# An RWKV and attention hybrid layer on one core: the triangular inverse before the power, the output pool in another place, attention's units in another order

## The chip, the core and the metric

The kernel runs on one core of a Trainium2 chip. TensorE (PE; its weight loads are PEld) multiplies, VectorE (DVE), ScalarE (ACT) and GpSimd (POOL) do the rest, SyncE (SP) issues most of the DMAs. Each engine takes its own instructions in the order that was fixed when the program was built. The metric is the device time of one execution in microseconds; the median of three runs before the change is 2141.12 us (2139.89 to 2146.02).

## The reference

One layer on x of 2048 tokens by 1024, in f32, and a last norm:

```
xn = rmsnorm(x);  p = xn @ w_in                  # 1024 -> 3076 columns
# RWKV-7, 8 heads of 64: one state S (64x64) per head, token after token
S = S*w_t + (S @ -kk_t) (kk_t*a_t)^T + v_t k_t^T;   y_t = S r_t
y_rwkv = (groupnorm(y) + (r.k.r_k) v) * silu(gate)
# sparse attention, 8 heads: an indexer scores all earlier keys,
# the best 256 of each query are kept, softmax over these
score = sum_h w_h relu(qi_h . ki);  idx = top_k(score, 256)
y_attn = softmax(q . c[idx]) @ c[idx], through w_uk, w_uv, * silu(gate)
out = rmsnorm(x + concat(y_rwkv, y_attn) @ w_out)
```

## The kernel before

Four stages, each a Python function; the program is unrolled.

`phase_as` does the projections (three f32r products for each f32 one) and the picker, which writes one mask per query block to DRAM. It is not touched.

`phase_r` does the RWKV heads. Tokens are taken in 16 batches of 128, each of two chunks of 64 (`o` = 0, 1); the heads stand side by side. A batch n goes through
- `prep` (twice, for two halves of the heads): loads, decays on VectorE, the products `E` of the chunk with itself, masked by VectorE (L978); at its end GpSimd scales `BK` (L988), queued behind the last operation of an inverse (`scaled_after`);
- `systems`: the triangular systems in `E` go through DRAM (`du`, L1016) into `A` (L1018), which has one buffer;
- `inverse`: GpSimd inverts them in 31 steps of two operations on `Xr` and `Xtmp` (L1032, L1034); `Xr` goes through DRAM (`dx`, L1035) into `TT` (L1039);
- `chain`, for each `o`: TensorE reads the state, ScalarE copies, TensorE solves with `TT` (L1069) in two steps, and VectorE writes the next state `S` (L1097); `y` is copied (L1098);
- `tail_norm`: the group norm of y on VectorE and ScalarE, with a power on GpSimd (`gst`, L1113) and a last multiply on VectorE (L1114); `tail_out`: transposes, `yo` on ScalarE and GpSimd (L1127 to L1130), a store to `d_y`.

In the loop over n the order of the source is: `tail_norm` of batch n-1, `inverse` of n+1 (queued on GpSimd behind that power), the first `prep` of n+2, `chain(n, 0)`, `tail_out` of n-1, second `prep` of n+2 and its `systems`, `chain(n, 1)`.

`phase_t` does the attention: for each of 4 pairs of heads p, 16 query blocks b, one unit each. `scores` makes the scores of a unit in chunks of 512 keys (L1262, L1263; VectorE adds the mask and takes the maximum, L1264; ScalarE exponentials, L1271), and beside it `attend` does the unit before: transposes (L1295), copies (L1297), products with the values (L1304), times the gate (L1317), then a store. A unit b has b+1 key tiles of 128; a head pair has 136, all four 544. Units run b = 0 to 15. A chunk of keys is loaded when the first unit needs it (`b % 4 == 0`), queries for two blocks at a time.

`phase_w` does the output: weights split into `wh` and `wl`, then 16 blocks of 128 tokens: load `yl`, copy to `yh`, difference, 48 products of 512 columns (L1377 to L1380), the sum with x, the norm, the store.

A planner sets the order on each engine at build time: an instruction goes in when its operands are ready by the planner's own estimate, the lowest priority number first. `with later(n)` adds to that number: the chain comes first, the rest of `phase_r` next, attention behind that with `later(2)`, the output with `later(3)`. `with tc.issue_after(x)` queues what it holds behind `x` on `x`'s engine. Tiles lie in pools, left and right; a pool that takes the place of another waits for its tiles. Before the change attention (pool `pT`) takes the left place when the picker's pool is closed, and the output (`pW`) takes `pT`'s place:

```
        with ExitStack() as sl:
            env["pa"], env["ps"] = pools(sl, "pT", "left")
            with later(2):
                phase_t(env)
        env["pa"], env["ps"] = pools(left, "pW", "left")
```

Of the kernel before, what the change touches and what calls it, by code (L numbers as in the profile page):

```python
# [20 lines left out]
NB = 16  # L21
# [3 lines left out]
NP = 4  # L25
# [11 lines left out]
def kernel(ctx: ExitStack, tc: tile.TileContext, x, norm_g, w_in, mu_shift, w0, w_up, a0, a_up,  # L37
# [109 lines left out]
    with ExitStack() as left, ExitStack() as right:  # L147
        env = dict(locals())
        with ExitStack() as sl:
            env["ps_"], env["pss"] = pools(sl, "pS", "left")  # L150
            with ExitStack() as sr:
                env["pa"], env["ps"] = pools(sr, "pX", "right")
                phase_as(env)
            sr = right.enter_context(ExitStack())
            if "R" in stages:
                env["pr"], env["psr"] = pools(sr, "pR", "right")
                phase_r(env)
        with ExitStack() as sl:
            env["pa"], env["ps"] = pools(sl, "pT", "left")
            with later(2):  # L160
                phase_t(env)
        env["pa"], env["ps"] = pools(left, "pW", "left")
        V.tensor_reduce(any_bad, bad, axis=AX.X, op=OP.max)
        rows = env["ps"].tile([128, 512], F32, name="rows", tag="po", bufs=3)
        PE.matmul(rows[0:1, 0:1], any_bad, ones1, start=True, stop=True)
        V.tensor_scalar(flag, rows[0:1, 0:1], 0.5, None, op0=OP.is_gt)
        with later(3):
            phase_w(env)
    redo = nc.values_load(flag, min_val=0, max_val=1)
    with tc.If(redo > 0):  # L170
        again(env)
# [716 lines left out]
def phase_r(env):  # L888
# [43 lines left out]
    def prep(tq, i, eC, scaled_after):  # L932

        sl = slice(tq * W, tq * W + W)
        u = NS(dict(ps=(i, 2 + i), sl=sl, i=i))
        ld = tl([128, 5, NC, C], F32, "ld", 2)
        u.vt = tl([128, 2, C + W], F32, "vt", 4)
        dma(ld.rearrange("p q (g o) c -> p q g (o c)", g=2),
            e.d_rw.rearrange("p q (g i) t -> p q g i t", i=2)[:, :, :, i, sl])
        v = e.d_v4.rearrange("p (g i) t -> p g i t", i=2)[:, :, i]  # L940
        if tq:
            dma(u.vt, v[:, :, tq * W - C:tq * W + W])
        else:
# [24 lines left out]
        V.tensor_tensor(u.X[:, :, 1], r, eL[:, :, 1:], op=OP.mult)  # L968
        u.E = tl([128, 2, NC, 2 * C], F32, "E", 6)
        mk = mask[:, i].rearrange("p a b -> p (a b)")[:, None, :].to_broadcast([128, NC, 2 * C])  # L970

        pe = [pst([128, NC, 2 * C], "rp", 2) for h in range(2)]
        for c in range(NC):
            for h in range(2):
                PE.matmul(pe[h][:, c], u.BK[HALF[h], c].rearrange("p a b -> p (a b)"),  # L975
                          u.X[HALF[h], c].rearrange("p a b -> p (a b)"), start=True, stop=True)
        for h in range(2):
            V.tensor_tensor(u.E[:, h], pe[h], mk, op=OP.mult)  # L978
        for p, hf in zip(u.ps, half):
            V.scalar_tensor_tensor(r[:, hf], r[:, hf], e.rkc[:, p:p + 1], k[:, hf], op0=OP.mult, op1=OP.mult)  # L980

        pb = pst([128, 2, W], "rp", 2)
        PE.matmul(fl(pb), fl(hsum), fl(u.r), start=True, stop=True)
        u.bv = tl([128, 2, W], F32, "bv", 6)
        V.tensor_tensor(u.bv, pb, u.vt[:, :, C:], op=OP.mult)
        bk = u.BK.rearrange("p c a b -> p c (a b)")
        with tc.issue_after(scaled_after):
            G.tensor_tensor(bk, bk, u.eC[:, :, None].to_broadcast([128, NC, 2 * C]), op=OP.mult)  # L988
        return u
# [127 lines left out]
    def tail_out(us, y):  # L1117
# [2 lines left out]
        for c in range(NC):  # L1120
            PE.transpose(pt[:, c].rearrange("p a b -> p (a b)"), y[:, c], ident)
        for i, u in enumerate(us):
            yo = tl([128, 2, W], F32, "yo", 3)
            gr = tl([128, 2, W], F32, "gr", 2)
            dma(gr, e.d_gr4.rearrange("p (g i) t -> p g i t", i=2)[:, :, u.i, u.sl])
            for g, p in enumerate(u.ps):
                S.activation(yo[:, g].rearrange("p (a b) -> p a b", a=2), pt[:, 2 * g:2 * g + 2, i], AF.Identity,  # L1127
                             scale=e.gng[:, p:p + 1], bias=e.gnb[:, p:p + 1])
            G.tensor_tensor(yo, yo, u.bv, op=OP.add)
            G.tensor_tensor(yo, yo, gr, op=OP.mult)  # L1130
            dma(e.d_y.rearrange("p (g i) t -> p g i t", i=2)[:, 0:2, u.i, u.sl], yo)
# [28 lines left out]
    for n in range(N):  # L1160
        b = batch.pop(n)
        new = batch[n + 2] = begin(n + 2) if n + 2 < N else None
        nx = batch.get(n + 1)
        norm = None
        with e.later():
            if b0:
                norm = tail_norm(y0)
            if nx:
                with behind(norm):
                    nx.TT, first = inverse(nx.A)  # L1170
            if new:
                with behind(state):
                    new.us.append(prep(n + 2, 0, new.eC, first))
        y = tl([128, NC, 128], F32, "y", 2)
        state = chain(b.us, b.TT, b.eC, y, n, 0)
        with e.later():
            if b0:
                tail_out(b0.us, y0)
            if nx:
                for u in nx.us:  # L1180
                    prep2(u)
            if new:
                with behind(state):
                    new.us.append(prep(n + 2, 1, new.eC, first))
                new.A = systems(new.us)
        state = chain(b.us, b.TT, b.eC, y, n, 1)
        y0, b0 = y, b
    with e.later():
        tail_norm(y0)
# [3 lines left out]
def phase_t(env):  # L1193
# [23 lines left out]
    def chunk_in(p, c):  # L1217
# [6 lines left out]
        dma(v, e.d_vt[:, 4 * c:4 * c + 4, p])  # L1224
        KT[p, c], VT[p, c] = k, v

    def queries_in(p, c):

        Q[p, c] = []
        for i in range(2):  # L1230
            q = tl([128, 2, 256], F32R, f"q{i}", 2)
            for s in range(2):
                dma(f32(q)[HALF[s]], e.d_q[i][:, p, c * 256:c * 256 + 256].rearrange("(h d) t -> d h t", h=2))
            Q[p, c].append(q)

    def load(p, b):

        if b % 4 == 0:
            chunk_in(p, b // 4)
        if b % 2 == 0:  # L1240
            queries_in(p, b // 2)
        mk = MK[p, b] = tl([128, T], BF16, "mk", 3)
        dma(mk[:, :(b + 1) * 128], e.d_mask[b])
        ga = GA[p, b] = tl([128, 128], F32, "ga", 5)
        return dma(ga, e.d_ga[p][:, b * 128:b * 128 + 128]).ins

    def scores(p, b, out):

        n = (b + 1) * 128
        mk = MK.pop((p, b))  # L1250
        qs = slice(b % 2 * 128, b % 2 * 128 + 128)
        qh, ql = Q[p, b // 2]
        rows = [tl([128, T], F32, "sc", 4) for h in range(2)]
        mx = tl([128, 2, 8], F32, "mx", 3)
        sums = tl([128, 2], F32, "sums", 3)
        for nt, c0 in enumerate(range(0, n, C)):
            w = min(C, n - c0)
            wp = max(w, 256)
            k = KT[p, nt]
            for h in range(2):  # L1260
                pS = pst([128, C], "s", 2)
                PE.matmul(pS[:, :wp], qh[:, h, qs], k[:, h, :wp], start=True, stop=False)  # L1262
                PE.matmul(pS[:, :wp], ql[:, h, qs], k[:, h, :wp], start=False, stop=True)  # L1263
# [4 lines left out]
        nt = (n + C - 1) // C  # L1268
        for h in range(2):
            V.tensor_reduce(mx[:, h, 4:5], mx[:, h, :nt], axis=AX.X, op=OP.max, negate=True)  # L1270
            S.activation(rows[h][:, :n], rows[h][:, :n], AF.Exp, bias=mx[:, h, 4:5], accum_out=sums[:, h:h + 1])  # L1271
        out.extend((rows, sums))

    def attend(p, b, rows, sums):
# [42 lines left out]
        V.tensor_tensor(ga, ga, po, op=OP.mult)  # L1317
        stores.append((e.d_y[:, 4 + p, ts], ga))

    units = [(p, b) for p in range(NP) for b in range(NB)]  # L1320
    last, stores = None, []
    load(*units[0])
    for i, u in enumerate(units + [None]):
        out = []
# [14 lines left out]
    for x in stores:  # L1339
        dma(*x)  # L1340


def phase_w(env):
# [18 lines left out]
    for tb in range(NB):  # L1362
# [2 lines left out]
        yr = tl([128, 8, 128], F32, "yl", 2)  # L1365
        yl = yr.bitcast(F32R)
        dma(yr, e.d_y[:, :, ts])
        S.activation(yh, yr, AF.Copy)  # L1368
        V.tensor_tensor(yl, yr, f32(yh), op=OP.subtract)
        xr = tl([128, D], F32, "xr", 2)  # L1370
        dma(xr, e.x[0, ts, :])
# [44 lines left out]
```

## Time and profile before

| | |
|---|---|
| median of three runs | 2141.12 us |
| the profiled execution | 2145.71 us, span 2144.0 us |
| busy: PE, PEld, DVE, ACT, POOL | 1818.9, 1435.7, 1313.2, 1022.5, 800.7 us |
| mean granted TensorE clock | 0.901 |
| up to about 975 us | projections and picker |
| 975 to 1843 us | RWKV heads, attention between them |
| 1843 to 1938 us | the rest of attention |
| 1957 to 2144 us | output |

Times are microseconds from the start of the span. L1069 is line 1069 of the kernel. Busy times of TensorE contain modelled ends, so packed products overlap in them. In the chain of waits each row is what the work stood on at that time; "issue" is time for which the profile shows no cause.

### The profile page before, as it was taken

Reading aid. Unit: us, or ns where it says so; the run is one execution under the profiler, and the core shown is the slowest. Engines: PE = TensorE matmul, PEld = TensorE weight load, DVE = VectorE, ACT = ScalarE, POOL = GpSimd, SP = SyncE. Lnnn points to the kernel's source line nnn. Section 1 sums busy time; section 2 is a strip of 40 time slices with the busy share of each in tenths; the row PEclk is TensorE's granted clock in tenths of the full one; section 3 lists DMA queues with packets and bytes.
Section 4 is the critical chain, followed back from the end, with each engine's and each line's share of the span. In section 5 each row is a group of like instructions: output and inputs, shape, how many; then the busy total and the mean of one; then the engine's idle time right before and its main releaser. Section 6 shows DMA issues by size and latency. Waiting matters only on the chain.

```text
span 2144.0 us, 36181 instructions
## 1 busy us (share of the span) xinstructions
PE 1818.9 (85%) x12906; PEld 1435.7 (67%) x12906; DVE 1313.2 (61%) x3050; ACT 1022.5 (48%) x1966; POOL 800.7 (37%) x1925
## 2 busy tenths in 40 slices
PE   5798998789797988895797977898787888996998
PEld 4676776568575766774576755677566666775886
DVE  5533539879697988985475665665466563543332
ACT  5323593444535654332364653556445555663221
POOL 1100233452545355541555554544455454100000
PEclk9788999989898999997898997999688897998999
DMA  7536243233352433227643553335433433214443
GB/s 252 187 135 200 66 136 126 81 110 95 112 181 78 138 125 118 90 83 182 169 113 97 129 147 92 106 98 145 115 105 95 108 93 101 85 39 162 145 148 110
DMA packets 309038, 262.50 MB, mean 122 GB/s; under 512 B 82544, under 2 KB 258288, under 8 KB 307696
## 3 DMA queue, kind: packets, MB, share of 16 engines
q1 hardware_dynamic: 304464, 248.03, 39.6%
q0 software_dynamic: 4384, 12.06, 1.7%
q8 instruction: 104, 1.70, 0.3%
q14 instruction: 86, 0.70, 0.1%
HBM read 166.37 MB, written 97.85 MB: 123 GB/s over the span
## 4 chain that ended last, share of the span: by engine, by line
PE 26%; DMA 11%; POOL 9%; issue 7%; DVE 4%; ACT 2%; SPq 1%; POOLq 0%; DVEq 0%; ACTq 0%
DMA dx<-Xr 5%; PE tr L1295 4%; PE om L1304 3%; POOL Xr L1034 3%; POOL Xtmp L1032 3%; PE po L1377 3%; PE po L1378 3%; PE po L1380 3%; PE s L1262 2%; PE s L1263 2%; DMA TT<-dx 2%; PE ch L1069 1%; DMA q<-d_q 1%; PE rp L975 1%; DMA d_y<-ga 1%
## 5 line engine op out<-in xcount | busy, mean ns | idle before, releaser
L578 PE MATMUL pm<-xh,wh 128*128 128x512 f32 x800 | 327.8, 410 | 19.8 <-DVE t L589 10.5
L579 PE MATMUL pm<-xl,wh 128*128 128x512 f32 x800 | 324.6, 406 | 0.0
L580 PE MATMUL pm<-xh,wl 128*128 128x512 f32 x800 | 324.1, 405 | 0.0
L1264 DVE CUSTOM_DVE_ANT_0 sc<-s,mk 128x512 f32<-128x512 f32 (+3 forms) x320 | 188.7, 607 | 161.2 <-PE s L1263 127.6
L1297 ACT ACTIVATE pt<-tr 128x512 f32<-128x512 f32 (+1 forms) x288 | 158.4, 570 | 142.2 <-PE tr L1295 81.6
L578 PEld LDWEIGHTS pm<-xh,wh 128*128 128x128 f32 x800 | 156.6, 196 | 60.7 <-DVE t L589 12.7
L1295 PE MATMUL tr<-ident,sc 128*128 128x128 f32 x1088 | 182.4, 295 | 8.5 <-ACT pt L1297 7.5
L579 PEld LDWEIGHTS pm<-xl,wh 128*128 128x128 f32 x800 | 156.5, 196 | 35.1
L580 PEld LDWEIGHTS pm<-xh,wl 128*128 128x128 f32 x800 | 155.9, 195 | 35.7
L1304 PE MATMUL om<-pt,vt 128*64 128x128 f32 x2176 | 172.8, 296 | 7.4 <-DVE ga L1287 7.3
L1271 ACT ACTIVATE sc<-sc,mx 128x128 f32<-128x128 f32 (+15 forms) x128 | 153.0, 1197 | 36.5 <-DVE mx L1270 35.9
L1032 POOL TENSOR_TENSOR Xtmp<-Xr,A 128x60 f32<-128x60 f32 (+24 forms) x496 | 148.6, 300 | 55.3 <-DMA A<-du 18.1
L1262 PE MATMUL s<-kt,q 128*128 128x512 f32 (+2 forms) x320 | 152.2, 477 | 17.4 <-DVE mx L1264 13.2
L1034 POOL TENSOR_TENSOR Xr<-Xr,Xtmp 128x60 f32<-128x60 f32 (+24 forms) x496 | 149.0, 300 | 37.1
L1295 PEld LDWEIGHTS tr<-ident,sc 128*128 128x128 f32 x1088 | 134.2, 150 | 40.1 <-issue 12.8
L1304 PEld LDWEIGHTS om<-pt,vt 128*64 128x64 f32 x2176 | 134.8, 147 | 35.2 <-issue 17.0
L318 ACT ACTIVATE mk<-x,st 128x1920 bf16<-128x1920 f16 (+5 forms) x72 | 98.0, 1361 | 105.1 <-POOL st L315 105.0
L250 ACT ACTIVATE rl<-lg,wi 128x512 f32<-128x512 f32 (+3 forms) x152 | 94.1, 631 | 100.3 <-PE lg L248 51.7
L1263 PE MATMUL s<-kt,q 128*128 128x512 f32 (+2 forms) x320 | 126.8, 398 | 7.8 <-DMA q<-d_q 7.7
L1069 PE MATMUL ch<-R,TT 32*32 32x64 f32 x1024 | 53.3, 242 | 92.0 <-DMA TT<-dx 91.6
L321 DVE TENSOR_SCALAR_CACHE_REDUCE mk<-x,st 128x2048 bf16<-128x2048 f16 (+5 forms) x72 | 120.6, 1676 | 1.4
L1377 PE MATMUL po<-wh,yh 128*128 128x512 f32 x256 | 100.9, 394 | 19.4 <-ACT yh L1368 19.4
(329 smaller groups left out, 3899.5 us busy)
## 6 DMA issues: line engine op xcount, KB each, us to landing
wraw<-in_w_in_dram SPq DMA_DIRECT2D x42, 512.0 KB
d_rw<-t SPq DMA_DIRECT2D x80, 256.0 KB
ld<-d_rw SPq DMA_DIRECT2D x32, 640.0 KB
q<-d_q SPq DMA_DIRECT2D x128, 128.0 KB
d_q<-t SPq DMA_DIRECT2D x32, 256.0 KB
d_kt<-t SPq DMA_DIRECT2D x32, 256.0 KB
kt<-d_kt SPq DMA_DIRECT2D x32, 256.0 KB
A<-du SPq DMA_DIRECT2D x16, 512.0 KB
```

Of the source, the lines that this page charges most:

```text
L578: PE.matmul(pm, wh[:, k], XH[g][:, k], start=k == 0, stop=False)
L579: PE.matmul(pm, wh[:, k], XL[g][:, k], start=False, stop=False)
L580: PE.matmul(pm, wl[:, k], XH[g][:, k], start=False, stop=k == KD - 1)
L1032: G.tensor_tensor(tmp[:, :m, :w], Xr[:, :m, s:s + 1].to_broadcast([128, m, w]), A[:, s:s + 1, s + 1:].to_broadcast([128, m, w]), op=OP.mult)
L1034: m_ = G.tensor_tensor(Xr[:, :m, s + 1:], Xr[:, :m, s + 1:], tmp[:, :m, :w], op=OP.add)
L1262: PE.matmul(pS[:, :wp], qh[:, h, qs], k[:, h, :wp], start=True, stop=False)
L1263: PE.matmul(pS[:, :wp], ql[:, h, qs], k[:, h, :wp], start=False, stop=True)
L1264: V.tensor_tensor_reduce(out=rows[h][:, c0:c0 + w], in0=pS[:, :w], in1=mk[:, c0:c0 + w], scale=1.0, scalar=LOW, op0=OP.add, op1=OP.max, ac ...
L1295: PE.transpose(pt[:, i, h], rows[h][:, (kb + i) * 128:(kb + i) * 128 + 128], ident)
L1297: S.activation(w[:, :m], pt[:, :m], AF.Copy)
L1304: PE.matmul(po[HALF[h]], v[:, (kb + i) % 4, HALF[h]], w[:, i, h], start=kb + i == 0, stop=kb + i == b)
L1377: PE.matmul(po, yh[:, m], wh[:, m, ds], start=m == 0, stop=False)
```

## The change

Three edits.

1. In `phase_r`'s loop the inverse of n+1 comes first, and `tail_norm` of n-1 behind it: its power is queued on GpSimd behind the inverse's last operation. `tail_out` of n-1 moves behind `chain(n, 1)`. `bv` gets 8 buffers for 6, `yo` 2 for 3.
2. The output's pool takes the right place, that of `phase_r`, closed when the RWKV heads are done; attention's pool stays open on the left. `phase_t` returns marks: for block b, the exponential of the unit that stands four behind unit b of the last head pair; `phase_w` queues the copy `yh` of block b on ScalarE behind it.
3. Units of a head pair run b = 15, 0, 14, 1, ..., 8, 7. All four key chunks are loaded with unit 15, the last chunk first, and `scores` goes through the chunks from the last to the first. Queries are loaded for each block by itself, three buffers.

```diff
-        with ExitStack() as sl:
-            env["pa"], env["ps"] = pools(sl, "pT", "left")
-            with later(2):
-                phase_t(env)
-        env["pa"], env["ps"] = pools(left, "pW", "left")
+            sr = ExitStack()
+            env["pr"], env["psr"] = pools(sr, "pR", "right")
+            phase_r(env)
+            sr.close()
+        env["pa"], env["ps"] = pools(left, "pT", "left")
+        with later(2):
+            behind = phase_t(env)
+        env["pa"], env["ps"] = pools(right, "pW", "right")
...
         with e.later():
-            if b0:
-                norm = tail_norm(y0)
             if nx:
-                with behind(norm):
-                    nx.TT, first = inverse(nx.A)
+                nx.TT, first = inverse(nx.A)
+            if b0:
+                with behind(first):
+                    tail_norm(y0)
...
         state = chain(b.us, b.TT, b.eC, y, n, 0)
         with e.later():
-            if b0:
-                tail_out(b0.us, y0)
             if nx:
...
         state = chain(b.us, b.TT, b.eC, y, n, 1)
+        with e.later():
+            if b0:
+                tail_out(b0.us, y0)
...
     def load(p, b):
-        if b % 4 == 0:
-            chunk_in(p, b // 4)
-        if b % 2 == 0:
-            queries_in(p, b // 2)
+        queries_in(p, b)
...
+        last = dma(ga, e.d_ga[p][:, b * 128:b * 128 + 128])
+        if b == NB - 1:
+            for c in reversed(range(4)):
+                last = chunk_in(p, c)
+        return last.ins
...
-        for nt, c0 in enumerate(range(0, n, C)):
+        for nt, c0 in reversed(list(enumerate(range(0, n, C)))):
...
-    units = [(p, b) for p in range(NP) for b in range(NB)]
+    units = [(p, b) for p in range(NP) for i in range(NB // 2) for b in (NB - 1 - i, i)]
...
+    at = {b: i for i, (p, b) in enumerate(units) if p == NP - 1}
+    return {b: marks[units[at[b] + 4]] for b in at if at[b] + 4 < len(units)}
...
-        S.activation(yh, yr, AF.Copy)
+        with tc.issue_after(behind[tb]) if tb in behind else ExitStack():
+            S.activation(yh, yr, AF.Copy)
```

## Rows read from the trace of the kernel before

**Rows 1.** The page: busy us, share of the span, instructions of each engine

```profile
PE 1818.9 (85%) x12906; PEld 1435.7 (67%) x12906; DVE 1313.2 (61%) x3050; ACT 1022.5 (48%) x1966; POOL 800.7 (37%) x1925
```

**Rows 2.** Busy time by stage: stretch, length, each engine (instructions), clock, DMA, GB/s

```profile
975.00:1060.00 85.00, 53.26 (x313) 39.60 (x313) 48.08 (x163) 28.82 (x79) 24.46 (x77) 0.74 0.82 192
1060.00:1843.00 783.00, 670.48 (x7389) 523.58 (x7389) 449.08 (x1364) 426.78 (x976) 390.94 (x1108) 0.87 0.43 110
1843.00:1938.00 95.00, 89.56 (x815) 67.66 (x813) 46.01 (x172) 61.72 (x113) 4.50 (x5) 1.00 0.18 50
...
1957.40:2144.00 186.60, 176.17 (x768) 145.41 (x768) 61.02 (x64) 39.08 (x79) 15.02 (x48) 0.98 0.39 129
```

**Rows 3.** Waits of 1060 to 1845 us: engine, line, releaser, us, times, longest

```profile
POOL gst L1113 <- DVE gst L1112: 207.9, 15, 22.0
...
PE ch L1069 <- DMA TT<-dx: 91.6, 15, 9.6
POOL yo L1129 <- ACT yo L1127: 82.9, 12, 14.4
```

**Rows 4.** Chain of waits: start us, us, what (first, one middle, last batch)

```profile
1059.84 1.64 DMA TT<-dx
...
1558.45 11.27 DMA dx<-Xr
1570.59 1.89 DMA TT<-dx
1572.53 1.05 PE ch L1069 x14
...
1586.48 0.43 DVE S L1097
...
1594.66 0.57 PE ch L1069 x16
...
1607.07 20.48 issue
...
1811.26 1.83 DMA TT<-dx
```

**Rows 5.** GpSimd's groups, 1060 to 1843 us: times, busy us, mean ns, idle before

```profile
L1032 POOL TENSOR_TENSOR Xtmp<-Xr,A 128x60 f32<-128x60 f32 (+24 forms) x465 | 139.0, 299 | 34.9
...
L1113 POOL TENSOR_TENSOR gst<-gst,mhalf 128x8 f32<-128x8 f32 x15 | 24.8, 1656 | 207.9 <-DVE gst L1112 207.9
```

**Rows 6.** Timelines of SyncE and GpSimd: the load of A, and its first use

```profile
1005.38 0.63 SPq L1018 DMA_DIRECT2D A<-du  x1
...
1017.94 0.24 POOL L1032 TENSOR_TENSOR Xtmp<-Xr,A 128x31 f32<-128x31 f32 x1 [18.14 <-DMA A<-du]
...
1607.39 2.35 SPq L1018 DMA_DIRECT2D A<-du  x1
```

**Rows 7.** TensorE's groups of attention: 1060 to 1843, then 1843 to 1940 us

```profile
L1295 PE MATMUL tr<-ident,sc 128*128 128x128 f32 x828 | 140.2, 297 | 3.1 <-ACT pt L1297 2.6 <-ACT sc L1271 0.5
...
L1295 PE MATMUL tr<-ident,sc 128*128 128x128 f32 x218 | 34.0, 280 | 4.6 <-ACT pt L1297 4.5
```

**Rows 8.** Chain of waits, 1500 to 2150 us: packed products of attention and output

```profile
1885.88 0.87 PE tr L1295 x8
...
1899.16 1.90 PE om L1304 x32
...
2126.33 1.81 PE po L1380 x8
```

**Rows 9.** Timeline of the seam between attention and output

```profile
1937.94 0.29 DVE L1317 TENSOR_TENSOR ga<-ga,om 128x128 f32<-128x128 f32 x1 [6.16 <-PE om L1304]
...
1957.42 0.79 PE L1377 MATMUL po<-wh,yh 128*128 128x512 f32 x1 [19.40 <-ACT yh L1368]
```

**Rows 10.** The page: DMA issues of the key loads, times and KB each

```profile
kt<-d_kt SPq DMA_DIRECT2D x32, 256.0 KB
```

**Rows 11.** Line 1233 (query loads): duration ns min/median/max, first and last start us

```profile
L1233 SPq DMA_DIRECT2D q<-d_q x128: 573/599/2451, 982.6 to 1877.3; - x128
```

More of the change, by code (lines that the diff above doesn't have):

```diff
@@ L153 @@
                 phase_as(env)
[L154 to L157, printed above, removed]
-        with ExitStack() as sl:
-            env["pa"], env["ps"] = pools(sl, "pT", "left")
-            with later(2):
-                phase_t(env)
-        env["pa"], env["ps"] = pools(left, "pW", "left")
+            sr = ExitStack()
[6 more added lines that the diff above has]
+        env["pa"], env["ps"] = pools(right, "pW", "right")
         V.tensor_reduce(any_bad, bad, axis=AX.X, op=OP.max)
@@ L167 @@
         with later(3):
-            phase_w(env)
+            phase_w(env, behind)
     redo = nc.values_load(flag, min_val=0, max_val=1)
@@ L983, in prep @@
         PE.matmul(fl(pb), fl(hsum), fl(u.r), start=True, stop=True)
-        u.bv = tl([128, 2, W], F32, "bv", 6)
+        u.bv = tl([128, 2, W], F32, "bv", 8)
         V.tensor_tensor(u.bv, pb, u.vt[:, :, C:], op=OP.mult)
@@ L1122, in tail_out @@
         for i, u in enumerate(us):
-            yo = tl([128, 2, W], F32, "yo", 3)
+            yo = tl([128, 2, W], F32, "yo", 2)
             gr = tl([128, 2, W], F32, "gr", 2)
@@ L1163, in phase_r @@
         nx = batch.get(n + 1)
-        norm = None
         with e.later():
+            if nx:
+                nx.TT, first = inverse(nx.A)
             if b0:
-                norm = tail_norm(y0)
-            if nx:
-                with behind(norm):
-                    nx.TT, first = inverse(nx.A)
+                with behind(first):
+                    tail_norm(y0)
             if new:
@@ L1223, in chunk_in, with queries_in @@
         v = tl([128, 4, 128], F32, "vt", 5)
-        dma(v, e.d_vt[:, 4 * c:4 * c + 4, p])
         KT[p, c], VT[p, c] = k, v
-    def queries_in(p, c):
-        Q[p, c] = []
+        return dma(v, e.d_vt[:, 4 * c:4 * c + 4, p])
+    def queries_in(p, b):
+        Q[p, b] = []
         for i in range(2):
-            q = tl([128, 2, 256], F32R, f"q{i}", 2)
+            q = tl([128, 2, 128], F32R, f"q{i}", 3)
             for s in range(2):
-                dma(f32(q)[HALF[s]], e.d_q[i][:, p, c * 256:c * 256 + 256].rearrange("(h d) t -> d h t", h=2))
-            Q[p, c].append(q)
+                dma(f32(q)[HALF[s]], e.d_q[i][:, p, b * 128:b * 128 + 128].rearrange("(h d) t -> d h t", h=2))
+            Q[p, b].append(q)
     def load(p, b):
-        if b % 4 == 0:
-            chunk_in(p, b // 4)
-        if b % 2 == 0:
-            queries_in(p, b // 2)
+        queries_in(p, b)
         mk = MK[p, b] = tl([128, T], BF16, "mk", 3)
@@ L1250, in scores @@
         mk = MK.pop((p, b))
-        qs = slice(b % 2 * 128, b % 2 * 128 + 128)
-        qh, ql = Q[p, b // 2]
+        qh, ql = Q.pop((p, b))
         rows = [tl([128, T], F32, "sc", 4) for h in range(2)]
@@ L1261, in scores @@
                 pS = pst([128, C], "s", 2)
-                PE.matmul(pS[:, :wp], qh[:, h, qs], k[:, h, :wp], start=True, stop=False)
-                PE.matmul(pS[:, :wp], ql[:, h, qs], k[:, h, :wp], start=False, stop=True)
+                PE.matmul(pS[:, :wp], qh[:, h], k[:, h, :wp], start=True, stop=False)
+                PE.matmul(pS[:, :wp], ql[:, h], k[:, h, :wp], start=False, stop=True)
                 V.tensor_tensor_reduce(out=rows[h][:, c0:c0 + w], in0=pS[:, :w], in1=mk[:, c0:c0 + w],
@@ L1270, in scores @@
             V.tensor_reduce(mx[:, h, 4:5], mx[:, h, :nt], axis=AX.X, op=OP.max, negate=True)
-            S.activation(rows[h][:, :n], rows[h][:, :n], AF.Exp, bias=mx[:, h, 4:5], accum_out=sums[:, h:h + 1])
+            marks[p, b] = S.activation(rows[h][:, :n], rows[h][:, :n], AF.Exp, bias=mx[:, h, 4:5],
+                                       accum_out=sums[:, h:h + 1]).ins
         out.extend((rows, sums))
@@ L1318, in attend @@
         stores.append((e.d_y[:, 4 + p, ts], ga))
-    units = [(p, b) for p in range(NP) for b in range(NB)]
-    last, stores = None, []
+    units = [(p, b) for p in range(NP) for i in range(NB // 2) for b in (NB - 1 - i, i)]
+    last, stores, marks = None, [], {}
     load(*units[0])
@@ L1340, in phase_t, with phase_w @@
         dma(*x)
-def phase_w(env):
+    at = {b: i for i, (p, b) in enumerate(units) if p == NP - 1}
+    return {b: marks[units[at[b] + 4]] for b in at if at[b] + 4 < len(units)}
+def phase_w(env, behind={}):
     e = NS(env)
```

1 line of the change is left out of this document (removed).

## The prediction, on record before the changed kernel was seen

> **What bounds the kernel now.** I read the page's busy times first [rows 1], then busy time by stage [rows 2], then who waits for whom in the long middle stage [rows 3], then the chain of waits through one batch [rows 4] and the engines inside it [rows 5, 6], then attention's and the output's products [rows 7, 8], and last the seam between these two [rows 9].
>
> TensorE is busy 1818.9 us, more than any other engine [rows 1], but not for one reason. By stages [rows 2]: from 1060 to 1843 us (the RWKV batches with attention between them) it is busy 670 of 783 us; from 1843 to 1938 (attention alone) 89.6 of 95; from 1957.4 on it is full to the last 10 us. Projections and the picker, up to 975 us, hold nothing that the change touches.
>
> In the middle stage the largest wait is GpSimd's: 207.9 us in 15 waits of `gst`, the power of `tail_norm`. TensorE stands 91.6 us, 15 times, until the inverse `TT` lands, once for each batch from the second on [rows 3]. So every batch's first solve waits for its inverse. The chain of waits shows why [rows 4]: solve at 1572.53, state written at 1586.9, second solve at 1594.7; GpSimd is free at 1607.07 and stands 20.48 us for the power, behind which alone the next inverse starts. After an inverse come its store (11.27 us) and the load `TT` (1.89). From `TT` of the first batch at 1059.84 to that of the last at 1811.26 are 751.4 us for 15 batches: 50.1 us each. That period sets when the RWKV heads end (1843), since attention only fills between.
>
> **The change, part by part**
>
> *Inverse ahead of the power.* What leaves the loop is the way chain, `tail_norm`, power, inverse: the 207.9 us of waits, 13.9 per batch. What is late next, worked out from rows:
> - The inverse is 62 GpSimd operations of 0.30 us [rows 5] = 18.6; with its five memsets I take 19.5. It can start when the store of the one before has freed `Xr` (about 11.3 + 1) and `A` has come; `A` has one buffer and its load starts behind the last inverse. The one wait for `A` that shows ended 12.56 us after the issue (1005.38 to 1017.94) [rows 6]. GpSimd's own loop is then 19.5 + 1 + 12.6 = 33 us; the power (1.66 [rows 5]), two `BK` and four `yo` operations lie inside that 12.6.
> - From a state to the solve two batches on: `prep` follows the state of 1586.9 on VectorE, `A` is issued at 1607.39 [rows 4, 6], so 20.5; `A` 12.6; inverse 19.5; store and `TT` 14.2; solve to state 14.4 (1572.53 to 1586.9). Together 81 for two batches, 40.6 each.
> - The chain itself: 14.4 from a solve to its state and 7.7 from a state to the next solve [rows 4], twice in a batch: 44.
>
> So the chain becomes the limit at 44 to 46 us, and I take 45: 5 us in each of 14 batches (the first two don't change), 70 us off the RWKV heads' end, most of the 91.6 that TensorE stands. Not all of it reaches the end. If attention keeps its share per batch, the 70 count whole; if the planner, seeing a shorter batch, puts less of it between, attention is done later. Between them: TensorE's work in the middle stage, in packed times, is about 0.71 us for each key tile of attention (two transposes at 0.109, four `om` at 0.0594 [rows 8], scores about 0.26) times 414 tiles (828 transposes [rows 7]) = 294, and some 255 for the RWKV heads, 70% of 783 us. With 70% kept, the 70 us take 49 us of attention's work along, which costs 49 / 0.84 = 58 later (0.84: 109 tiles [rows 7], 78 us of packed work, with small products 80, in 95), and 12 are left. Ends: -12 and -92; I take -55, nearer to the whole, since the order on TensorE's queue is fixed beforehand and its waits are what shrinks.
>
> The second half of this edit (`tail_out` after the chain, `bv` with 8 buffers, `yo` with 2) issues the same instructions later; the GpSimd waits for `yo` (82.9 us [rows 3]) lie outside the new loop. At nothing; if the `yo` operations still stand inside the inverse, 5.5 us a batch stay in the 33-us loop, which has 11 to spare.
>
> *Output pool in the RWKV heads' place.* Weights are loaded and split, and blocks are multiplied, from the RWKV heads' end on, between attention's last units. Three things come of it. The seam of 19.5 us from attention's last product at 1937.94 to the first output product at 1957.42 [rows 9] goes but for 2: -17. The 8 loads, 8 copies and 8 differences of the weights then lie beside attention, whose ACT is busy 61.7 and DVE 46.0 of 95 us [rows 2]: nothing. And `behind` lets block b be copied after the exponentials of the fourth unit behind unit b; in the order 15, 0, 14, 1, ... that is units 5, 7, 9, 11, 13 and 15 of the last head for blocks 0 to 5. So 5.3 blocks can run before attention ends; a block is 48 products at 0.226 us (8 in 1.81 [rows 8]) = 10.9: 58 us. They gain only what TensorE has free there. By packed times some 16 of 95 us are free; the last head has 136 tiles, 119 us at attention's own speed (95 for 109): 20 to 22 us. Sum -39; ends -22 (by the busy column only 5.4 of 95 are free) and -75 (all 58 hidden, if the RWKV heads still run beside the last head).
>
> The Trainium skill ("Trainium Kernel Development and Optimization", Performance Expectations) warns that matmul busy time overstates how full TensorE is and names weight-load busy time as the better measure. Here the two differ as it says, 89.6 against 67.7 of 95 us [rows 2]; by weight loads 27 are free, 34 in 119, and the sum would be 12 us lower.
>
> *Long and short units in turn, keys from the last chunk.* The work is the same. A first unit now needs four chunks instead of one: keys of three more, 6 loads of 256 KB [rows 10], 8 us at the 192 GB/s of that stretch [rows 2]; its scores start on the chunk that comes first, so +6. At each of three changes of head chunks 1 and 0 wait for unit 7's scores, and the next unit needs them at once: 1 MB of keys at 110 GB/s [rows 2] is 9.5 us, of which the products of unit 7 cover 8 tiles x 0.46 = 3.7: +5.8, and TensorE's queue stands with it; +17 for three, less the 5 to 7 us that a change of head costs now by the same path: I take +10 for all three. Queries are 256 loads instead of 128 of half the size, 0.6 us of SyncE's queue each [rows 11]: 77 us more in 950, spread, hidden as long as SyncE is not behind; if it is, what stands behind them are `du`, `A` and the store of the inverse. Turn about of long and short: nothing, within 15 us either way. Sum +16; ends 0 and +45.
>
> *Sum.* -55 - 39 + 16 = -78. The profiled execution took 2145.7 us (span 2144.0 and 1.7 around it), so 2067.7; the median of the runs, 2141.12, is 4.6 lower: 2063. Its own range, from neighbouring values of the terms, is 2030 to 2100.
>
> **Rivals**
>
> A. *Given back.* The batch gets shorter and attention falls behind by as much: -12 - 39 + 16 = -35, 2106. For it: packed work fills only 70% of the middle stage today, and the planner places attention by its own estimate of the batch, not by the 11.27 us that a store took [rows 4]. Against: the wait that goes is one in which the whole TensorE queue stands.
>
> B. *All hidden.* -92 - 75 + 6 = -161, 1980. For it: at 44 us a batch holds 16.5 us of RWKV and 18.6 of attention work. Against: the chain's own waits stay.
>
> C. *Slower: VectorE waits for the power.* The power now stands behind the whole inverse on GpSimd, and behind it VectorE's last multiply of `tail_norm`. If that multiply stands ahead of `prep`'s instructions in VectorE's queue, a loop closes: inverse 19.5, power 1.7, the multiply, `prep` to `du` and `A` 20.5, load 12.6: 55 us, in each batch. That is +70 for 14, with -39 and +16: +47, 2188. It decides from 51.7 us a batch (where 14 x 1.6 eat the 23 us of the rest). For it: `prep` on VectorE starts right at the state, and an inverse begun 33 us (20.5 + 12.6) behind the state of the batch before ends 53 behind it, when the next state, 45 behind, is already there. Against: VectorE has no wait for the power now, and the planner places the multiply when it believes the power done. The Trainium skill ("TensorE: Matmul & The Clock Gate", Architectural detail) says that VectorE's, ScalarE's and GpSimd's queues are strictly first in, first out; GpSimd's 207.9 us agree, and by that rule alone this rival would hold wherever the planner is early.
>
> D. *The output stage stays behind.* If its products are planned after attention's anyway, only -55 + 16 remain, less a few us at the seam: 2100.
>
> **How the numbers follow.** Chances: forecast 50%, A 20%, B 11%, C 9%, D 6%; 4% that the terms cancel. A measurement of this kernel tells 0.3%, 6.4 us, from no change. Forecast, B and nearly all of A and D are faster; C is slower: faster 86%, same 4%, slower 10%. The range leaves out B's lower half and C with a few of A: 2005 to 2125.
>
> **What would show it.** First step: GpSimd's wait for `gst` is gone, TensorE's wait for `TT` falls under 35 us, and batches come every 44 to 46 us. Second: the first output product runs before attention's last, five or six blocks lie before it, no idle stretch of 19 us is left. Third: at changes of head TensorE waits for keys, under 10 us each. Wrong would be a period of 50 or more, a wait of VectorE for GpSimd's power over 3 us a batch, or output products that stand for `yh` with attention behind them.

## The result, and the profile after

Slower, by half a per cent. The changed kernel takes 2152.31 us (median of 6 runs) against 2142.36 for the kernel before (6 runs): a ratio of 1.0052, interval 1.0034 to 1.0070. The prediction was 2063, with 2005 to 2125 as its range: wrong in sign, and outside the range.

The page's busy times are those of before within 1.2% [rows 1]: the work is the same. The granted TensorE clock does not explain the loss: 0.904 on the mean, against 0.901 before. Times are of one profiled execution with a span of 2151.2 us.

```profile
PE 1822.3 (85%) x12906; PEld 1427.0 (66%) x12906; DVE 1298.5 (60%) x3050; ACT 1016.9 (47%) x1966; POOL 792.8 (37%) x1925
```

Busy time by stage, as in [rows 2]. The columns are stretch, length, PE, PEld, DVE, ACT, POOL (instructions), clock, DMA share, GB/s.

```profile
1060.00:1754.00 694.00, 585.78 (x6806) 456.03 (x6807) 400.70 (x1213) 375.04 (x873) 382.01 (x1104) 0.88 0.45 111
1754.00:2035.00 281.00, 253.31 (x1746) 188.73 (x1744) 118.98 (x388) 139.09 (x285) 13.59 (x29) 0.96 0.38 114
2035.00:2151.00 116.00, 99.67 (x432) 82.07 (x432) 35.68 (x37) 22.57 (x45) 9.06 (x29) 0.93 0.38 124
```

The RWKV heads end at 1754, 90 us earlier than before [rows 2]: more than the 70 forecast. Edit 1 alone gives 60 of them (`f1_inverse_only`, below), and with edit 3 alone they end 32 us earlier (`f3_order_only`). Then come 281 us in which attention and output share TensorE, and 116 us of output alone.

The waits of 1060 to 1754 us, as in [rows 3]: engine, line, releaser, us, times, longest.

```profile
POOL Xtmp L1031 <- DMA A<-du: 158.4, 13, 18.2
DVE y L1113 <- POOL gst L1112: 76.7, 14, 10.6
...
PE ch L1068 <- DMA TT<-dx: 31.4, 7, 10.0
DVE sc L1263 <- PE tr L1295: 30.2, 7, 8.6
```

GpSimd no longer waits for `gst` (207.9 us before); its largest wait is now the load of `A`, 12.2 us each time. TensorE waits 31.4 us for `TT`, not 91.6. VectorE now waits 76.7 us for the power, 5.5 each time: rival C's sign. But its loop did not close. The four `TT` loads of the first batch and of the last, from SyncE's timeline (start us, us):

```profile
1063.08 1.86 SPq L1038 DMA_DIRECT2D TT<-dx  x4
...
1719.11 1.80 SPq L1038 DMA_DIRECT2D TT<-dx  x4
```

That is 656.0 us for 15 batches, 43.7 each, where the chain of before had 50.1 [rows 4] and the forecast 45.

So the first edit did what it was to do for the RWKV heads. What attention did meanwhile is seen by counting its products `om`, four to a key tile, 2176 (544 tiles) in all. The view is busy time by windows for line 1304 on TensorE alone; the count in brackets is what is read. First before, then after:

```profile
0.00:1750.00 1750.00, 122.49 (x1508) 0.89 0.43 124
1750.00:1860.00 110.00, 22.77 (x268) 0.88 0.39 105
1860.00:2035.00 175.00, 27.58 (x400) 0.94 0.34 112
```

```profile
0.00:1750.00 1750.00, 113.41 (x1400) 0.89 0.43 124
1750.00:1860.00 110.00, 27.39 (x368) 0.94 0.53 152
1860.00:2035.00 175.00, 26.91 (x408) 0.98 0.28 87
```

By 1750, 377 tiles were through before and 350 after: the RWKV heads are ahead and attention is behind. Faster heads alone do not explain that: in `f12_old_order`, below, they end at 1777, and 374 tiles are through by 1750. From 1860 to 2035 attention takes the whole stretch again, since the output now shares TensorE with it. The same view for the last third of the output's products (L1385, eight to a half block):

```profile
0.00:1860.00 1860.00, 0.00 (x0) 0.90 0.44 125
1860.00:2035.00 175.00, 29.44 (x112) 0.98 0.28 87
2035.00:2200.00 165.00, 35.57 (x144) 0.95 0.27 87
```

14 of 32 half blocks are done at 2035; 18 stand behind attention. The seam there, on TensorE's, VectorE's and ScalarE's timeline (start us, us; in brackets idle time before and its releaser), answers to [rows 9]:

```profile
2030.68 1.97 PE L1304 MATMUL om<-pt,vt 128*64 128x128 f32 x32
...
2038.88 1.06 ACT L1373 ACTIVATE yh<-yl 128x1024 fp32r<-128x1024 f32 x1 [4.32 <-DMA yl<-d_y]
...
2039.99 0.80 PE L1382 MATMUL po<-wh,yh 128*128 128x512 f32 x1 [6.91 <-ACT yh L1373]
```

### The profile page after: what moved, and what is told of

Its sections match the earlier page's. It is cut to its first block, busy times and chain, and to the rows that moved or that the text cites. A ratio compares the mean times of both kernels' runs of the same rounds, so it can differ in the third digit from the quotient of the medians.

```text
span 2151.2 us, 36412 instructions
## 1 busy us (share of the span) xinstructions
PE 1822.3 (85%) x12906; PEld 1427.0 (66%) x12906; DVE 1298.5 (60%) x3050; ACT 1016.9 (47%) x1966; POOL 792.8 (37%) x1925
## 4 chain that ended last, share of the span: by engine, by line
PE 20%; POOL 14%; DMA 12%; issue 5%; DVE 4%; ACT 3%; SPq 2%; POOLq 0%; ACTq 0%; DVEq 0%
POOL Xr L1033 6%; POOL Xtmp L1031 6%; DMA A<-du 5%; PE po L1382 3%; PE po L1383 3%; PE po L1385 3%; PE tr L1295 3%; PE om L1304 2%; DMA dx<-Xr 2%; ACT sc L1270 2%; DMA TT<-dx 1%; PE s L1261 1%; DMA vt<-d_vt 1%; DVE sc L1263 1%; DMA wl<-d_wo 1%
## 5 line engine op out<-in xcount | busy, mean ns | idle before, releaser
L1261 PE MATMUL s<-kt,q 128*128 128x512 f32 (+2 forms) x320 | 149.1, 467 | 42.9 <-DVE mx L1263 32.6
L1270 ACT ACTIVATE sc<-sc,mx 128x2048 f32<-128x2048 f32 (+15 forms) x128 | 152.8, 1195 | 53.6 <-DVE mx L1269 53.2
L1304 PE MATMUL om<-pt,vt 128*64 128x128 f32 x2176 | 167.7, 293 | 2.7 <-DMA vt<-d_vt 1.7
L1304 PEld LDWEIGHTS om<-pt,vt 128*64 128x64 f32 x2176 | 132.2, 146 | 31.6 <-issue 22.0
L1262 PE MATMUL s<-kt,q 128*128 128x512 f32 (+2 forms) x320 | 125.5, 394 | 9.9 <-DMA q<-d_q 9.9
```

Of the source, the lines that this page charges most:

```text
L1261: PE.matmul(pS[:, :wp], qh[:, h], k[:, h, :wp], start=True, stop=False)
L1270: marks[p, b] = S.activation(rows[h][:, :n], rows[h][:, :n], AF.Exp, bias=mx[:, h, 4:5], accum_out=sums[:, h:h + 1]).ins
L1304: PE.matmul(po[HALF[h]], v[:, (kb + i) % 4, HALF[h]], w[:, i, h], start=kb + i == 0, stop=kb + i == b)
```

## The experiments

Fourteen kernels were run, in four sets. Each is compared with the kernel before, run beside it on the same chip; differences are worked out from the ratios, 1% being 21.4 us. The four below ran first, to tell the three edits apart.

**Each edit alone, and the first two together.** `f1_inverse_only` is edit 1 of the diff, `f2_pool_only` edit 2, `f3_order_only` edit 3, `f12_old_order` edits 1 and 2 with the units as they were. Against the changed kernel the last one has

```
-    units = [(p, b) for p in range(NP) for i in range(NB // 2) for b in (NB - 1 - i, i)]
+    units = [(p, b) for p in range(NP) for b in range(NB)]
...
-        for nt, c0 in reversed(list(enumerate(range(0, n, C)))):
+        for nt, c0 in enumerate(range(0, n, C)):
```

and its loads of keys and queries from before.

> Only the first edit: the inverse ahead of the power and tail_out behind the chain, attention and output as before. Theory O (the new order of units is what costs): the RWKV heads end some 85 us earlier, attention has its old order and speed (95 us for its last 109 tiles), so 2070 to 2105. Theory G (given back: attention falls behind by what the batch gets shorter, whatever its order): the RWKV heads end as early, but attention still has about 180 tiles to do then, and the total is 2125 to 2145. Theory W (the output blocks between the units cost) says nothing here but what is not lost in the other two: 2070 to 2105.

> Only the second edit: the output's pool in the RWKV heads' place, units in the old order, each copy yh behind the exponentials of the fourth unit after its own. The RWKV heads end at 1843 as before. Theory O: the seam of 19.5 us goes and a few blocks fill gaps, 2105 to 2125. Theory W: each block that stands between units makes TensorE wait for yh and for the exponentials, some 5 us a block, so 2135 to 2160. Theory G: as O, 2105 to 2125.

> Only the third edit: units 15, 0, 14, 1, ... and keys from the last chunk, inverse and output as before. Theory O: attention alone goes at about 1.1 us a key tile, as between 1754 and 1815 us in the changed kernel, instead of 0.87, so 2160 to 2190. Theories G and W: 2135 to 2150, no difference.

> The changed kernel with units in the old order (first and second edit). Theory O: attention after the RWKV heads runs at its old speed with output blocks between its units, 2045 to 2090. Theory G: 2100 to 2120. Theory W: 2130 to 2160, close to the changed kernel's 2152.

| run | median us | ratio to before | interval | us |
|---|---|---|---|---|
| f1_inverse_only | 2125.14 | 0.9913 | 0.9886 to 0.9941 | -19 |
| f2_pool_only | 2124.45 | 0.9920 | 0.9882 to 0.9957 | -17 |
| f3_order_only | 2169.00 | 1.0134 | 1.0077 to 1.0190 | +29 |
| f12_old_order | 2096.15 | 0.9793 | 0.9735 to 0.9852 | -44 |
| the change | 2152.31 | 1.0052 | 1.0034 to 1.0070 | +11 |

Edits 1 and 2 are gains and add up; the 8 us over lie within the intervals. Edit 3 costs 29 alone and 55 on top of the two: theory O of this set, the order of the units, stands as to what costs, and part of its cost needs the other two edits. O's ranges held for f2 and f3; f1 misses its range by 20 us and f12 by 6, since the inverse gains less than O allowed. G's range held for the inverse, at its lower end; the gain of 19 is far under the forecast of 55, and of the 180 tiles that G left to attention 144 are measured. W falls, since the output pool alone gains. The profile of `f12_old_order`, the products `om` (L1304) and then the output's (L1385), in the windows used above:

```profile
0.00:1750.00 1750.00, 123.02 (x1498) 0.91 0.43 125
1750.00:1860.00 110.00, 22.43 (x282) 0.97 0.59 180
1860.00:2035.00 175.00, 26.46 (x392) 1.00 0.33 106
...
0.00:1860.00 1860.00, 8.64 (x32) 0.91 0.44 128
1860.00:2035.00 175.00, 42.76 (x152) 1.00 0.33 106
2035.00:2200.00 165.00, 17.78 (x72) 0.98 0.11 36
```

Attention's last gate multiply in `f12_old_order`, from VectorE's timeline:

```profile
2035.89 0.29 DVE L1317 TENSOR_TENSOR ga<-ga,om 128x128 f32<-128x128 f32 x1 [2.32 <-PE om L1304]
```

So attention ends at about the same place, 2035.9 against 2032.7. But 23 half blocks lie before it (184 products of L1385), where the changed kernel has 14. Nine halves of 5.44 us (24 packed products each) are 49 us, and the changed kernel's seam of 7 makes 56: the loss, read at one point. Part of it is there at 1777, when the RWKV heads are done in both kernels and no output product has run. The products `om` by then, of the changed kernel and of `f12_old_order`:

```profile
0.00:1777.00 1777.00, 120.40 (x1496) 0.89 0.43 124
...
0.00:1777.00 1777.00, 130.84 (x1600) 0.91 0.43 125
```

That is 374 tiles against 400. The rest comes after. Busy time by stage (columns as above) from 1777 to 2035, again of the changed kernel and of `f12_old_order`:

```profile
1777.00:2035.00 258.00, 232.12 (x1571) 172.95 (x1569) 104.74 (x334) 122.40 (x249) 5.88 (x20) 0.96 0.37 110
...
1777.00:2035.00 258.00, 248.02 (x1603) 195.74 (x1601) 118.95 (x311) 121.18 (x242) 18.08 (x42) 0.99 0.42 133
```

TensorE stands idle for 25.9 of these 258 us in the changed kernel, for 10.0 in the other.

**Which part of edit 3.** Four runs on the changed kernel:

```
g1_descending      units b = 15, 14, ... 0, and the output's loop over tb likewise
g2_output_in_turn  -    for tb in range(NB):
                   +    for tb in [b for i in range(NB // 2) for b in (NB - 1 - i, i)]:
g3_keys_forward    chunks loaded and scored 0 to 3, units in turn
g4_ascending_loads units 0 to 15, chunks 0 to 3, all four asked for with unit 0, queries by block
```

> Of the changed kernel only the order of a head's units is other: 15, 14, ... 0 in place of 15, 0, 14, 1, ..., and the output blocks are taken 15 to 0; loads by four chunks at the change of head and keys from the last chunk stay. Theory S (long and short in turn make the stages uneven, scores of a long unit lie beside a short unit's attend and the reverse, and four score rows are two units, so nothing evens it out): at the last state some 48 units' worth of tiles scored as in the kernel before, and 2095 to 2115 us. Theory O (the output goes by blocks 0 to 15 while the turn brings the long units back first): the same here, since the output follows the units, 2095 to 2115. Theory L (four chunks and a block's queries at the change of head cost the time): the gaps of 18 to 40 us at the changes of head stay and the time stays over 2135.

> The changed kernel with one line other: the output blocks are taken in the order in which the units come back, 15, 0, 14, 1, ..., not 0 to 15. Theory O: in the changed kernel 13 of 32 half blocks were done at attention's end and 19 stood behind it at 5.44 us each, since block 7 comes back last but one; here 24 or more are done by then, and the time is 2100 to 2120 us. Theory S: attention itself ends late (2033) and its stages stay uneven; the output that is now ready earlier fills idle TensorE time only in part, 2125 to 2145. Theory L: the loss lies at the changes of head before this, as S here, 2130 to 2145.

> The changed kernel with the key chunks loaded and scored from the first to the last again; units long and short in turn and the rest as changed. Theories S, O and L without the direction: within 8 us of the changed kernel's 2152. If the direction itself costs (the last, partly masked chunk first, and the four chunks' buffers given back in that order): 2130 or less. If it is what the turn needs: over 2160.

> The kernel with edits 1 and 2 and the old order of units (2096 us) plus the loads of edit 3 alone: four chunks asked for at a head's first unit, queries by a block of 128, keys first to last, units 0 to 15. Theories S and O: within 10 us of that kernel, 2090 to 2106. Theory L: most of the 56 us between that kernel and the changed one is back, 2130 to 2150.

| run | median us | ratio to before | interval | us against the change |
|---|---|---|---|---|
| g1_descending | 2101.79 | 0.9812 | 0.9755 to 0.9868 | -51 |
| g2_output_in_turn | 2126.56 | 0.9918 | 0.9892 to 0.9944 | -29 |
| g3_keys_forward | 2143.24 | 0.9997 | 0.9973 to 1.0022 | -12 |
| g4_ascending_loads | 2100.17 | 0.9812 | 0.9760 to 0.9863 | -51 |

(In this set and the next, S, O, L, B and P are as these texts say; O is now the order of the output's blocks.) Theory L falls: with the loads of edit 3 and the units in the old order (g4) the time is that of `f12_old_order`, 0.9812 against 0.9793 within their intervals. The order of the units is the cost: descending, with the same loads and the keys backward (g1), is as good. Theory O holds for 29 us, but g2 lies 7 us over its range and in that of S: O is not the whole. In the changed kernel the output takes blocks 0, 1, 2, ..., but blocks 8 to 15, whose long units come back among the first, must stand behind block 7, whose unit is the head's last. Between g2 and g1 only the order of the units is other, with the output following it in both: 23 us are left for the turn itself. The keys' direction costs 12 in the turn, 4 more than the 8 allowed, and 11 again between h2 and h3 below; in g1, where they also run backward, no cost of it is seen. Why it costs in the turn alone is open.

The profile shows where most of the 23 lie. The RWKV heads end at 1784 in g1 and at 1748 in g2, so tiles are compared at 1784, when they are done in both and no output product has run. The products `om` by then, of g1 and of g2:

```profile
0.00:1784.00 1784.00, 128.60 (x1608) 0.90 0.43 125
```

```profile
0.00:1784.00 1784.00, 122.04 (x1536) 0.90 0.43 125
```

402 tiles against 384: 18 behind, some 16 us at attention's own speed (95 us for 109 tiles [rows 2, 7], an estimate). In turn, attention gets less done beside the RWKV heads, and their earlier end does not make up for it. How a pair of units goes in the changed kernel shows in the last head's timeline (start us, us; in brackets idle time before and its releaser). Unit 13 is in `attend`, unit 12 in `scores`:

```profile
1878.63 0.66 PE L1295 MATMUL tr<-ident,sc 128*128 128x128 f32 x4
...
1879.21 0.29 DVE L1263 CUSTOM_DVE_ANT_0 sc<-s,mk 128x128 f32<-128x128 f32 x1 [1.68 <-PE tr L1295]
...
1880.65 0.48 PE L1261 MATMUL s<-kt,q 128*128 128x512 f32 x1
...
1886.53 1.69 ACT L1270 ACTIVATE sc<-sc,mx 128x1664 f32<-128x1664 f32 x1 [2.40 <-DVE mx L1269]
...
1888.22 1.67 ACT L1270 ACTIVATE sc<-sc,mx 128x1664 f32<-128x1664 f32 x1
...
1890.03 0.88 PE L1295 MATMUL tr<-ident,sc 128*128 128x128 f32 x6 [0.73 <-ACT sc L1270]
...
1891.29 1.04 ACT L1373 ACTIVATE yh<-yl 128x1024 fp32r<-128x1024 f32 x1
...
1892.39 0.50 PE L1382 MATMUL po<-wh,yh 128*128 128x512 f32 x1 [1.48 <-ACT yh L1373]
```

VectorE may write a score row of unit 12 (1664 columns) only when the last transposes of unit 13 have read the row whose buffer it takes: `sc` has four buffers, two rows to a unit. So the long unit's scores start when the transposes of the long unit before are done, beside a short unit's few products; then come 3.4 us of its exponentials, the next short unit's, the copy `yh`, and TensorE has little left. From 1889.3, when the last score product ends, to 1892.4 it runs six transposes.

**The score rows.** Is that the cause, or does the turn put the RWKV heads ahead in some other way? Two more rows were given to the short units, so that a long unit need not wait for the long unit two before it. For this three buffers were trimmed: first the trim alone (h1), then with the rows (h2, h3). The edit of h2 against g2:

```
-        rows = [tl([128, T], F32, "sc", 4) for h in range(2)]
+        if b < NB // 2:
+            rows = [tl([128, T // 2], F32, "ss", 2) for h in range(2)]
+        else:
+            rows = [tl([128, T], F32, "sc", 4) for h in range(2)]
...
     (h1, h2, h3)  masks: 2 long and 1 short buffer for 3;  "q0", "q1": 2 for 3;  "vt": 4 for 5
```

h3 is h2 with the keys forward; `h4_inverse_and_order` is edits 1 and 3 of the diff, without edit 2.

> The run with the output in turn (2126.6 us, units 15, 0, 14, 1, ...), with three buffers trimmed and nothing given: masks in 2 long and 1 short buffer for 3 long, queries 2 for 3, values 4 for 5. It is the foil of the next run. All theories: 2122 to 2140, 0 to 13 us worse for the loss of lookahead in the loads.

> As h1, and the room is spent on two score rows of 1024 for the short units, beside the four of 2048 that now only long units use, so that a long unit can be scored while the short one before it is not yet attended. Theory B (four rows hold two units, so in turn the scores of a long unit wait for the long unit before it, and its attend runs beside a short unit's scores alone): by 1750 some 370 to 380 of 544 tiles are through, as in the runs with the old or the descending order (374 to 380), where the turn had 350 to 352; time 20 to 30 us under h1, 2095 to 2112. Theory P (the turn puts the RWKV part ahead by its place in the instruction order, whatever the buffers): 350 tiles at 1750 and within 8 us of h1.

> As h2, and the keys from the first chunk to the last again. By the run with keys forward alone (2143.2 against 2152.3 for the changed kernel) it is 0 to 10 us under h2: 2088 to 2108. Theory P: 2115 to 2130.

> Edits 1 and 3 without edit 2: the output pool stands where it was, so that no output block can come before attention's end and the order of the blocks can cost nothing. If the turn costs two things that add, some 25 to 30 us in the stages and 26 us in the output's order: the first alone is added to the inverse alone (2125.1), 2148 to 2155. If the turn costs mainly through the output: 2120 to 2135. If it collides with the earlier inverse: over 2165.

| run | median us | ratio to before | interval |
|---|---|---|---|
| h1_turn_trimmed | 2145.94 | 1.0004 | 0.9987 to 1.0022 |
| h2_turn_six_rows | 2108.06 | 0.9829 | 0.9794 to 0.9865 |
| h3_rows_keys_forward | 2095.56 | 0.9779 | 0.9753 to 0.9805 |
| h4_inverse_and_order | 2157.65 | 1.0065 | 1.0042 to 1.0087 |

The rows give 38 us back (1.75%), more than the 20 to 30 expected: B's range for the time holds, P's does not. The rows' own expectation, 370 to 380 tiles, is missed by 2, and the trim cost more than its 0 to 13, 18 us. In the profile the products `om` up to 1750, of h1 and h2, go from 340 to 368 tiles:

```profile
0.00:1750.00 1750.00, 112.04 (x1360) 0.90 0.42 123
```

```profile
0.00:1750.00 1750.00, 122.79 (x1472) 0.90 0.43 124
```

At 1773, when the RWKV heads are done in both, it is 364 against 388 (1454 and 1551 products). The waits of VectorE for a row, 1060 to 1750 us, of h1 and then h2:

```profile
DVE sc L1267 <- PE tr L1299: 27.6, 7, 8.8
```

```profile
DVE ss L1270 <- PE tr L1302: 6.6, 3, 6.0
```

The wait for a long row is gone. It is a sign only: g1 has 27.2 us of it too and is fast, so the sum of these waits does not price the order; the tiles done by a time do. And it is one pair of kernels: below, another trade of buffers moves the time by 24 us, so that the rows are the cause of the 38 is likely, but how much of it is theirs is not shown. h3 is the best in turn and no better than `f12_old_order` (0.9779 and 0.9793 within their intervals). h4 is 33 us over `f1_inverse_only`, near the 29 of edit 3 alone, as the expectation of two costs that add has it (2148 to 2155, missed by 3): without edit 2 the output's order seems to cost nothing.

**Room for the rows.** TensorE's waits in h1, 1060 to 1750 us:

```profile
PE s L1265 <- DMA q<-d_q: 57.4, 11, 8.9
...
PE s L1266 <- DMA q<-d_q: 32.1, 8, 10.8
```

So the trim seemed to cost through the queries, 89.5 us in all. k1 is h3 with three buffers of queries, k2 is h3 with five of values; both pay with `pt`, three buffers for four.

> As h3 (six score rows, keys forward, 2095.6), but the queries have their three buffers again and the packed weights of the attention three for four. If the 19 us that the trim cost in h1 are the waits of the scores for the queries (TensorE 57.4 and 32.1 us in h1's stretch of both stages): the waits for the queries fall under 15 us, and 2072 to 2092, below every run so far. If the packed weights' fourth buffer is worth as much: 2093 to 2110.

> As h3, but the values have their five buffers again, the queries stay at two, and the packed weights have three for four. If the trim's cost lies with the queries: no better than h3, 2093 to 2108, and 10 us or more over k1. If it lies with the values at the changes of head: 2072 to 2092.

k1: 2121.18 us (0.9893, 0.9851 to 0.9934). k2: 2103.35 (0.9800, 0.9754 to 0.9846). The expectation of k1 missed: TensorE has no wait for queries left (35 us in h3, 1060 to 1750), and k1 is 24 us slower than h3 by the ratios. k2 lies in the range it had if the cost is the queries', but 18 us under k1, where it should have been over it. TensorE's waits in that stretch are 104 us in all in h3 and 107 in k1: in place of the queries it stands longer for VectorE's `E` (28.4 for 19.6) and `mx` (19.1 for 8.4). The loss shows in the tiles through by 1750, 384 and 368. So queries that come in time did not buy time here. k1 and k2 differ in queries and values alone, and the values' fifth buffer goes with the faster. Whether the fourth `pt` or the way in which the planner laid out these kernels makes up the rest is open; no run has the six rows with nothing taken away.

## Why the prediction was wrong

The step that failed is "Turn about of long and short: nothing, within 15 us either way". Edit 3 was put at +16 for its loads and changes of head, with the order free. Measured, it is +55 behind the other two. The loads, on which the +16 rested, cost nothing that can be told (g4 against `f12_old_order`, +4 us by the ratios, within the intervals). The order cost by two ways that I did not follow: the output's loop, which takes blocks in their own order while the units come in another (29 us, g2), and the score rows, which hold two units and so tie a long unit's scores to the last transposes of the long unit before. The turn itself is 23 us (g2 against g1); that the rows are its cause rests on the timeline and on one pair of kernels, where six rows give 38 back. With +55 in place of +16 the sum would have been -39.

The larger part of the miss, 50 of 89 us, is in the first two terms: -94 was forecast for them together, and `f12_old_order` measured -44.

*Inverse, -55; measured -19.* For the RWKV heads mechanism and period were right: in `f1_inverse_only` the batches come every 44.6 us (45 forecast), the last state is written 60 us earlier (70 forecast), and TensorE's wait for `TT` is 32.9 us in five. What failed is the step from there to the end. Rival A's "given back" is what happened, at 20%. Products `om` before and behind the RWKV heads' end, in the kernel before (1843) and in `f1_inverse_only` (1784):

```profile
0.00:1843.00 1843.00, 141.55 (x1716) 0.89 0.43 123
1843.00:2200.00 357.00, 31.30 (x460) 0.96 0.30 98
```

```profile
0.00:1784.00 1784.00, 132.15 (x1600) 0.90 0.43 125
1784.00:2200.00 416.00, 41.12 (x576) 0.96 0.30 97
```

115 tiles were left before and 144 in f1: 29 given back. The kernel before, at the same 1784 us:

```profile
0.00:1784.00 1784.00, 130.53 (x1594) 0.89 0.43 124
```

By then both have some 400 tiles through: attention kept its pace in time, not its share of a batch. Its last product in f1 falls at 1915.3 for 1937.9, 22.6 earlier, and the seam of 19.4 is unchanged:

```profile
1934.81 0.79 PE L1377 MATMUL po<-wh,yh 128*128 128x512 f32 x1 [19.39 <-ACT yh L1368]
```

Of the 60 us that the RWKV heads gained, 37 went: to the 29 tiles, and to a slower pace, 131 us for 144 tiles where 95 did for 115. Why the pace was slower is open. The reason "its waits are what shrinks" is what failed. TensorE's stage in f1, from 1060 to the last state:

```profile
1060.00:1784.00 724.00, 614.01 (x7155) 477.61 (x7155) 415.58 (x1281) 403.39 (x915) 382.08 (x1104) 0.89 0.44 112
```

It stands idle for 110.0 us there, and stood for 112.5 before, 1060 to 1843 [rows 2]: the wait for `TT` shrank by 59, the idle time as a whole did not. The second half of edit 1 (`tail_out` behind the chain, `bv`, `yo`), put at nothing, was not run apart, so what it adds or takes is not shown.

*Output pool, -39; measured -17.* The seam went, as said. The 20 to 22 us of output hidden in TensorE's free time did not come. The last unit's end in `f2_pool_only`, VectorE's timeline:

```profile
2022.57 0.29 DVE L1317 TENSOR_TENSOR ga<-ga,om 128x128 f32<-128x128 f32 x1 [3.05 <-PE om L1304]
```

By then 15 half blocks are done, 82 us of products, and attention ends 85 us later than before [rows 9]. Nothing was hidden, and the -17 measured is the seam's alone. Why none of the free time could be used is not shown. The Trainium skill ("Trainium Kernel Development and Optimization", Performance Expectations) calls matmul busy time a bad metric for how close a kernel is to roofline, and names the use of peak FLOPs and weight-load time as the good ones. The prediction read weight-load time as room for other work, 27 of 95 us, which the page does not say. None of it was had here, and the 5.4 that matmul busy time leaves free is the nearer.

*Rival C* showed its sign, 76.7 us of VectorE's waits for the power, and not its price: the period stayed at 43.7. The Trainium skill ("TensorE: Matmul & The Clock Gate", Architectural detail) has VectorE's queue as strictly first in, first out. The 5.5 us in each of 14 waits agree, but the loop of 55 did not close, and why it had room is not shown.

*The signs.* What I named for the three steps came nearly as said: the `TT` wait, the period (43.7, a little under the 44 to 46), the first output product before attention's end, seven blocks there for the five or six, and no wait for keys in TensorE's list. Two of the "wrong" signs came too: VectorE's 5.5 us a batch, and output products that stand for `yh` with attention behind them (6.5 us in 6 waits of 1815 to 2035). None of them was the measure of the loss. I had named no sign for how many tiles of attention are through at a given time, and that is what moved.

## What to carry to other kernels

When a fill-in stage shares an engine with a chain, a shorter chain is worth what the filler keeps: count the filler's work done by a time at which the chain is done in both kernels, and not the chain's period. A new order of unequal units is not free because the work is the same: check for each ring of buffers how many units it holds and which unit's end the next one waits for, and give every consumer that takes results in a fixed order the same new order. In a full TensorE stage, count work put between as pushing back the rest, unless a run shows the gap that takes it.

## What was not expected of the hardware

Trading one buffer for another moved a whole program, and the wait that went was replaced by others: k1, where TensorE has no wait for queries, is 24 us slower than h3, which stands 35 us for them in 1060 to 1750; its waits there are 107 and 104 us in all. And work put beside attention in the old order found no free time on TensorE: 15 output halves moved attention's end by 85 us, though by themselves they take 82.
